# Another order of banks, reads, taps and late low parts in the head and first triple of a short-convolution block

## The chip, the cores and the metric

One core of a Trainium2 chip runs the whole program. The metric is the device time of one execution in microseconds (us), the median of several runs; lower is better. The engines are named as in the profile: PE is TensorE's matrix multiplier and PEld its weight load, DVE is VectorE, ACT is ScalarE, POOL is GpSimd, and SP is SyncE, which only starts transfers here.

## The reference

The input x has 1024 rows of 1024 channels in float32. With DEPTH 1 only the short-convolution mixer runs, between two RMS norms:

```python
def rms_norm(x, g):
    xf = x.astype(jnp.float32)
    y = xf * lax.rsqrt(jnp.mean(xf * xf, axis=-1, keepdims=True) + EPS)
    return (y * g.astype(jnp.float32)).astype(x.dtype)

def short_conv_mixer(u, w_in, conv_w, w_out):      # w_in 1024 x 8192, conv_w 3 x 2048, w_out 2048 x 1024
    z, bg, cg, v = jnp.split(u @ w_in.astype(u.dtype), 4, axis=-1)
    y = bg * causal_dwconv(cg * v, conv_w) * jax.nn.silu(z)
    return y @ w_out.astype(u.dtype)

h = x
u = rms_norm(h, pre_norm[0])
h = h + rms_norm(short_conv_mixer(u, sc_w_in[0], sc_conv_w[0], sc_w_out[0]), post_norm[0])
```

`causal_dwconv` is a convolution over positions with three taps for each of the 2048 channels.

## The kernel before, in words

**Precision.** Every float32 operand of a matmul is split into a high part (rounded to the format that PE multiplies, by a copy on ScalarE) and a low part (the rest, by a subtraction on VectorE). A product is three passes: low weights by high data, high by low, high by high (`pass3`, lines 122 to 125). So each operand needs one ScalarE and one VectorE instruction for each half ahead of its product.

**Work.** The first projection has 64 groups of 128 columns: 16 channel blocks c, each with the types CG, V, Z and BG. The four groups of c = 0 (numbers 0 to 3: CG, V, Z, BG) are made by plain products in the head, `plain(n, h, ks)` for group n and half h of the 1024 positions. The other 60 groups go three at a time: 20 triples, each made by 20 products of combined weights and combined data in place of 24, with the combinations by additions. The products are numbered 0 to 19. The combined data of product i is `U[i]`, made once in the head and in triple 0 and kept for all triples; seven of them are plain blocks `B[g, h]` (g the quarter of the input channels, h the half of the positions), the others are sums of blocks, called forms here. The combined weights come from POOL's sixteen small steps `sums(t, steps)` and are split in pairs by ScalarE and VectorE: units A to J (`split_w`, lines 208 to 225), each for two products. After the triples comes the output projection.

**Order.** The order of the instructions on each engine is that of the program text; nothing is reordered, so an instruction that waits holds everything behind it on its engine. Tiles come from pools with a fixed number of slots. The next tile of a pool, in the order of the text, takes the slot that came free first, and its first write waits until the last user of the slot's former tile is done. Two pools matter: the eight PSUM banks (`bank`), and `up` with 18 slots for operands, each as large as one `U[i]`. Instructions of two engines on one bank follow each other in program order, reads too.

**The head (lines 603 to 763).** It norms x, turns it (`turn`, `turn2`: transposes into banks `pk`), splits each block (`read_k(k, h)`: ScalarE's line 479 the high part, VectorE's line 480 the low one), writes blocks back over x for the forms (`rebuild` on POOL, `rebuild_a` on ScalarE, line 489), and makes the forms. A form is held in two banks (`form`, `banks_of`) until its high part `high_u(i)` (line 559 from banks, 561 from a stage) and its low part `low_u(i)` (lines 567 and 569) are made, or is written to a stage. A stage is half a tile of the `up` pool (`PLACE` says which half of which tile); it keeps the forms 10, 4, 0, 16, 17 and 2 until there is time for their split in triple 0. Form 19's stage is a tile of the raw pool. `snap` copies a plain result out of its bank, group 2 with a Silu. `first_tap` and `other_taps` (lines 284 to 292) are the convolution of c = 0, on ScalarE and VectorE.

**Triple 0.** The loop at lines 828 to 863 goes through the steps s = 1 to 20. In each step come, in this order: the six matmuls of one product (`ORDER_0`: 7, 9, 1, 8, 3, 5, 14, 18, 0, 13, 17, 6, 4, 11, 15, 16, 10, 2, 12, 19); the reads of its bank into the three results (`read`, lines 334 to 355, a first read on ScalarE and later ones on VectorE); the low parts that are pending, first those of the splits and then those of the operands; the leftovers of c = 0 (`first_chunk`); in five steps the high part of the next operand of `LATE` (4, 16, 10, 2, 19), whose low part becomes pending; the split of a unit (`SPLIT_0` for this triple, `NEXT` for the coming one, A at step 15); and POOL's sums for the next triple. Products of one chain (`CHAINS`) add up in one bank, so a product waits until the reads of the product before it in its chain are done: 1, 5, 18, 11, 10, 12, 19 share bank pX; 9, 3, 17, 4, 15, 16 share pY; 7, 8, 14 share pV; 6 and 2 share pZ; 0 and 13 share pW.

Of the kernel before, what the change touches and what calls it, by code (L numbers as in the profile page):

```python
# [19 lines left out]
def kernel(  # L20
# [11 lines left out]
    nc = tc.nc  # L32
# [4 lines left out]
    NK = D // P  # L37
# [121 lines left out]
    def sums(t, steps):  # L159

        if t >= len(TRIPLES):
            return
        w0, w1, w2 = (ws[t, j] for j in range(3))
        if t not in es:
            es[t] = EP[t % 2].tile([P, 6, FC], F32, tag="e", name=f"e_{t}")
        e = es[t]
        add, sub = nc.gpsimd.tensor_add, nc.gpsimd.tensor_sub
        todo = {
            0: lambda: (add(w2[:, 0], w2[:, 0], w2[:, 1]), add(w2[:, 2], w2[:, 1], w2[:, 2])),  # L169
            1: lambda: sub(e[:, 0:2], w2[:, 0::2], w0[:, 0::2]),  # L170
            2: lambda: sub(e[:, 2], e[:, 1], w0[:, 3]),
            3: lambda: add(w1[:, 2], w2[:, 2], w1[:, 2]),
            4: lambda: sub(e[:, 3], w1[:, 2], w1[:, 0]),
            5: lambda: (sub(w0[:, 2], e[:, 3], w0[:, 2]), sub(w0[:, 0], e[:, 3], w0[:, 0])),  # L174
            6: lambda: sub(w0[:, 2], w0[:, 2], w0[:, 3]),
            7: lambda: sub(e[:, 4], w2[:, 1], w2[:, 3]),
            8: lambda: sub(e[:, 5], e[:, 4], w1[:, 3]),
            9: lambda: add(w2[:, 3], w1[:, 3], w2[:, 3]),
            10: lambda: sub(w1[:, 3], w1[:, 3], e[:, 2]),
            11: lambda: sub(w2[:, 3], e[:, 0], w2[:, 3]),  # L180
            12: lambda: sub(e[:, 3], e[:, 5], w1[:, 0]),  # L181
            13: lambda: add(w1[:, 0], w1[:, 0], w1[:, 1]),
            14: lambda: sub(e[:, 2], e[:, 0], w0[:, 3]),
            15: lambda: sub(w0[:, 3], w0[:, 3], w0[:, 1]),
        }
        for s in steps:
            todo[s]()
# [16 lines left out]
    def run_lows():  # L204
        while lows:
            lows.pop(0)()
# [39 lines left out]
    def inner(t):  # L246
        return t[:, TAPS - 1 :]
# [46 lines left out]
    def pad(c):  # L294
        nc.gpsimd.tensor_copy(gts[c, 1][:, : TAPS - 1], gts[c, 0][:, HB:])
# [177 lines left out]
    def read_k(k, h):  # L473

        g, kk = k // 2, k % 2
        if kk == 0:
            B[g, h] = new_u(f"b{g}{h}")
        u, src, gc = B[g, h], pk[k, h], gcol[:, k : k + 1]
        nc.scalar.activation(u[:, 0, kk], src, AF.Copy, scale=gc)
        nc.vector.scalar_tensor_tensor(u[:, 1, kk], src, gc, u[:, 0, kk].bitcast(F32), op0=ALU.mult, op1=ALU.subtract)  # L480
# [30 lines left out]
    def plain(n, h, ks):  # L511

        w = plain_w[n]
        for k in ks:
            first = (n, h) not in plain_ps
            if first:
                plain_ps[n, h] = bank(f"pp_{n}_{h}")
                plain_k[n, h] = 0
            plain_k[n, h] += 1
            hi, lo = (w[:, z, k * P : (k + 1) * P] for z in (0, 1))  # L520
            pass3(plain_ps[n, h], hi, lo, B[k // 2, h], k % 2, first, plain_k[n, h] == NK)

    def snap(n, h, gate=False):
        t = wide(snp, "sn", f"sp_{n}_{h}")
        if gate:
            gts[0, h] = t
        nc.scalar.activation(inner(t), plain_ps[n, h], AF.Silu if n == 2 else AF.Copy)
        return inner(t)
# [4 lines left out]
                turn(k, t)  # L533

    STAGE = {}
    PLACE = {10: (0, 0), 4: (0, 1), 0: (1, 0), 16: (1, 1), 6: (2, 0), 17: (2, 1), 11: (3, 0), 2: (3, 1)}

    def stage(i):
        if i == 19:
            if i not in STAGE:  # L540
                STAGE[i] = raw.tile([P, 2, HB], F32, tag="raw", name="s_19")
            return as_block(STAGE[i])
        n, j = PLACE[i]
        if n not in STAGE:
            STAGE[n] = up.tile([P, 2, 2, HB], F32, tag="u", name=f"s_{n}")
        return as_block(STAGE[n][:, j])
# [3 lines left out]
    def form(i, make, at=None):  # L550
        FORM[i] = at or [bank(f"f_{i}_{kk}") for kk in range(2)]
        for kk in range(2):
            make(by_tile(FORM[i][kk]), kk)

    def high_u(i):
        U[i] = u = new_u(f"u_{i}")
        for kk in range(2):
            if i in FORM:
                nc.scalar.copy(u[:, 0, kk], FORM[i][kk])
            else:  # L560
                nc.scalar.copy(as_block(u[:, 0])[:, kk], stage(i)[:, kk])
# [10 lines left out]
    def make(eng, dst, kind, a, b):  # L572

        for kk in range(2):
            d, x, y = (z[kk] if isinstance(z, list) else z[:, kk] for z in (dst, a, b))
            (eng.tensor_add if kind == "+" else eng.tensor_sub)(d, x, y)
# [12 lines left out]
    def turned(k, n, other, op):  # L589

        def do(dst, kk):
            nc.vector.scalar_tensor_tensor(dst, by_tile(pk[k + kk, 1]), n[:, k + kk : k + kk + 1], other[:, kk], op0=ALU.mult, op1=op)

        return do
# [74 lines left out]
    nc.scalar.mul(half_of(cw, 1), half_of(pc[:, : TAPS * NC], 1), -1.0)  # L669
    for k in (4, 5):  # L670
        read_k(k, 1)
    form(7, turned(4, gcol, b20, ALU.subtract))
    for k in (4, 5):
        rebuild_a(k, 1)
# [12 lines left out]
    low_u(5)  # L687
    high_u(8)
    low_u(8)
    plain(3, 0, range(NK))  # L690
    turn2((0, 1))
    for k in (0, 1):
        read_k(k, 1)
# [11 lines left out]
    plain(0, 1, (0, 1))  # L705
    turn2((2, 3))
    sn0[3] = snap(3, 0)
    for k in (6, 7):
        rebuild_a(k, 1)
    for k in (2, 3):  # L710
        read_k(k, 1)
    plain(1, 1, (0, 1))
    plain(0, 1, (6, 7, 2, 3))
    plain(1, 1, (6, 7, 2, 3))
# [15 lines left out]
    f6 = banks_of(6)  # L730
    make(nc.vector, f6, "-", b01, f19)
    high_u(6)
    make(nc.vector, stage(17), "+", f6, b30)
    nc.vector.tensor_mul(cv_of(0, 1), plain_ps[1, 1], cv_of(0, 1))
    f11 = banks_of(11)
# [3 lines left out]
    FORM.pop(19)  # L739
    FORM.pop("q")  # L740
    low_u(6)
    nc.gpsimd.tensor_mul(inner(gts[0, 0]), inner(gts[0, 0]), sn0[1])
    pad(0)
    head.close()
    EP[1] = mixed.enter_context(tc.tile_pool(name="ep1", bufs=1, reuse_waits="tile"))
    wp = mixed.enter_context(tc.tile_pool(name="wp", bufs=1, reuse_waits="tile"))
    tmp = mixed.enter_context(tc.tile_pool(name="tmp", bufs=1, reuse_waits="tile"))
    for unit in "ABCD":
        split_w(0, unit)
        run_lows()  # L750
        if unit == "B":
            low_u(11)
    sums(0, range(12, 16))
    for i in (0, 17):
        high_u(i)
        low_u(i, nc.gpsimd)
    first_tap(0, 0)
    first_tap(0, 1)
    other_taps(0, 0)
    other_taps(0, 1)  # L760
    silu1 = snap(2, 1)
    for i, (g, h) in ((1, (2, 1)), (3, (3, 0)), (14, (1, 0)), (13, (1, 0)), (18, (0, 0)), (15, (1, 1)), (12, (1, 1))):
        U[i] = B[g, h]
    LATE = [4, 16, 10, 2, 19]

    def first_chunk(s):

        if s == 3:
            for h, t in ((0, sn0[2]), (1, silu1)):
                nc.gpsimd.tensor_mul(cv_of(0, h), cv_of(0, h), t)  # L770
        elif s == 9:
            gate_y(0, 0, sn0[3], 1, False)
        elif s == 10:
            gate_y(0, 1, plain_ps[3, 1], 1, True)
# [46 lines left out]
    END = len(TRIPLES) - 1  # L821
    SUMS = {1: (0,), 2: (1,), 3: (2,), 4: (3,), 5: (4,), 6: (5,), 7: (6,), 8: (7,), 9: (8,), 10: (9,), 11: (10,), 12: (11,), 17: (12, 13), 18: (14,), 19: (15,)}
    SPLIT = {2: "E", 6: "F", 8: "G", 9: "H", 11: "I", 13: "J"}
    SPLIT_0 = {1: "F", 4: "G", 7: "H", 8: "E", 11: "I", 13: "J"}
    NEXT = {15: "A", 16: "B", 18: "C", 20: "D"}
    ORDER_0 = (7, 9, 1, 8, 3, 5, 14, 18, 0, 13, 17, 6, 4, 11, 15, 16, 10, 2, 12, 19)
    fetch_triple(1)
    for t in range(len(TRIPLES)):
        for s, i in enumerate(ORDER if t else ORDER_0, 1):
            now[0] += 1  # L830
            product(t, i)
            read(t, i)
            run_lows()
            while low_us:
                low_us.pop(0)()
            if t == 0:
                first_chunk(s)
                if s in (4, 7, 10, 12, 14):
                    n = LATE.pop(0)
                    high_u(n)  # L840
                    low_us.append(lambda n=n: low_u(n))
            run_due()
            for unit in (SPLIT if t else SPLIT_0).get(s, ""):
                split_w(t, unit)
            for unit in NEXT.get(s, ""):
                split_w(t + 1, unit)
            sums(t + 1, SUMS.get(s, ()))
            if s == 14:
                fetch_triple(t + 2)
            if s in (7, 14, 20):  # L850
                run_later()
            if 2 <= t < 2 + 2 * CH:
                j = (t - 2) // 2
                if t % 2 == 0 and s == 3:
                    fetch_t(j)
                if t % 2 == 0 and s == 15:
                    add_t(j, 0)
                if t % 2 == 1 and s in (15, 20):
                    add_t(j, 1 + (s == 20))
            if t == END - 1 and s == 14 or t == END and s in (2, 8, 13, 15, 17):  # L860
                fetch_unit()
            if t == END and s in (6, 9, 11, 13, 15, 17, 19, 20):
                split_unit(True)
# [150 lines left out]
```

## Time and profile before

| | |
|---|---|
| time, median of 3 runs | 778.89 us (777.88 to 779.18) |
| the profiled execution | 776.99 us, of which the span of the trace is 775.2 us |
| granted clock of PE over the span | 0.999 |
| head, 0 to 65.2 us of the span | PE busy 62.44 us, DVE 50.11, ACT 46.13, POOL 30.81 |
| triple 0, 65.2 to 97.4 us | PE busy 28.72 us, DVE 25.56, ACT 22.84, POOL 25.99 |
| the rest, 97.4 to 775.2 us | PE busy 670.61 us, DVE 410.54, ACT 382.09, POOL 401.61 |

How to read what follows: times in a view are microseconds from the start of the span, unless marked ns. A line number such as L569 is a line of the kernel before; where a helper issues an instruction, it is the helper's line. `x2` at the end of a timeline row means two instructions in a row that the view merged. `[0.54 <-DVE u L569]` says that the engine was idle for 0.54 us before the row, and that the semaphore that ended this came from DVE's line 569, which wrote a tile u. Tiles are named without their numbers: u are operands, b blocks, s stages, f forms in banks, wA to wJ the split weights, pX to pZ the banks of the chains.

### The profile page before, as it was taken

The page shows a single profiled execution, that of the slowest core. Times are in us where ns is not written, and L with a number is a line of the kernel's source. Part 1 is how long each engine was busy: PE and PEld are TensorE (multiplying, and loading weights), DVE is VectorE, ACT ScalarE, POOL GpSimd, SP SyncE. Part 2 cuts the span into 40 slices and gives each one's busy share as a digit, 9 for nine tenths or more (in the row PEclk, how much of TensorE's full clock was granted, in tenths as well). Part 3 has the DMA queues.
Part 4 walks back from the last instruction along what each step waited for, and adds up shares of the span by engine and source line. Part 5 has one row for each costly group of instructions (what it writes and reads, how often), then busy time and mean ns, then how long its engine had stood idle before and what let it go on. Part 6 is the DMA issues. An engine that isn't in the chain of part 4 may idle for free.

```text
span 775.2 us, 10034 instructions
## 1 busy us (share of the span) xinstructions
PE 761.8 (98%) x3394; PEld 628.3 (81%) x3394; DVE 486.2 (63%) x752; ACT 451.1 (58%) x877; POOL 458.4 (59%) x563
## 2 busy tenths in 40 slices
PE   9998999999999999999999999999999999999996
PEld 8786788888888888888888888888888888888885
DVE  6887866556566475656565665555665957544756
ACT  7859575556666565555665755565566636444531
POOL 0677688679679677776977887796874220000020
PEclk9999999999999999999999999999999999999999
DMA  9400424546436448266266466565544779754237
GB/s 335 128 1 28 135 67 153 120 136 151 108 109 162 128 105 213 59 179 134 82 150 176 106 155 133 138 163 109 150 93 133 232 247 378 280 186 176 93 121 259
DMA packets 103219, 116.55 MB, mean 150 GB/s; under 512 B 4680, under 2 KB 70272, under 8 KB 102144
## 3 DMA queue, kind: packets, MB, share of 16 engines
q1 hardware_dynamic: 93936, 99.13, 38.9%
q0 software_dynamic: 9216, 16.78, 13.9%
q8 instruction: 26, 0.43, 0.2%
q14 instruction: 25, 0.20, 0.1%
q10 hardware_dynamic: 16, 0.00, 0.0%
HBM read 97.02 MB, written 44.04 MB: 182 GB/s over the span
## 4 chain that ended last, share of the span: by engine, by line
PE 91%; ACT 5%; DVE 3%; issue 1%; DMA 0%; DVEq 0%; ACTq 0%
PE pX L123 8%; PE pX L125 8%; PE pX L124 8%; PE pY L123 7%; PE pY L125 7%; PE pY L124 7%; PE po_x L892 4%; PE po_x L893 4%; PE po_x L891 4%; PE pV L123 3%; PE pV L125 3%; PE pV L124 3%; PE pZ L125 2%; PE pZ L123 2%; PE pZ L124 2%; PE pW L125 2%
## 5 line engine op out<-in xcount | busy, mean ns | idle before, releaser
L931 POOL TENSOR_TENSOR res<-xr,res 128x512 f32<-128x512 f32 x4 | 6.9, 1720 | 105.5 <-DVE res L930 105.5
L329 POOL TENSOR_TENSOR g<-g,sn 128x512 f32<-128x512 f32 x29 | 40.2, 1391 | 45.5 <-ACT sn L327 35.2
L353 DVE TENSOR_TENSOR sn<-sn,pY 128x512 f32<-128x512 f32 x57 | 39.2, 688 | 36.2 <-PE pY L125 20.7
L353 DVE TENSOR_TENSOR sn<-sn,pX 128x512 f32<-128x512 f32 x57 | 39.2, 689 | 34.5 <-PE pX L125 34.5
L302 POOL TENSOR_TENSOR g<-sn,g 128x512 f32<-128x512 f32 x23 | 29.9, 1302 | 47.4 <-DVE sn L351 47.4
L327 ACT ACTIVATE sn<-sn 128x512 f32<-128x512 f32 x24 | 15.2, 633 | 64.1 <-DVE sn L353 40.1
L311 POOL TENSOR_TENSOR g<-g,sn 128x512 f32<-128x512 f32 x20 | 28.3, 1415 | 17.9 <-DVE sn L353 17.6
L345 ACT COPY sn<-pZ 128x512 f32<-128x512 f32 x19 | 11.2, 590 | 46.4 <-PE pZ L125 41.3
L347 ACT ACTIVATE sn<-pV 128x512 f32<-128x512 f32 x38 | 20.7, 600 | 28.5 <-PE pV L125 28.5
L169 POOL TENSOR_TENSOR raw<-raw 128x256 f32<-128x256 f32 x40 | 32.6, 933 | 0.0
L359 POOL DMA_DIRECT2D s_d<-s_d x24 | 19.8, 823 | 21.0 <-DMA s_d<-y_d 13.5
L174 POOL TENSOR_TENSOR raw<-e,raw 128x256 f32<-128x256 f32 x40 | 28.8, 741 | 1.6
L351 DVE TENSOR_TENSOR g<-pY,g 128x512 f32<-128x512 f32 x15 | 10.4, 692 | 30.7 <-PE pY L125 30.7
L123 PE MATMUL pp<-b,wn 128*128 128x512 f32 x64 | 26.0, 406 | 1.1 <-DVE u L567 1.0
L170 POOL TENSOR_TENSOR e<-raw,raw 128x512 f32<-128x512 f32 x20 | 25.9, 1295 | 1.6
L900 ACT ACTIVATE jk<-res 128x512 bf16<-128x512 f32 x12 | 7.6, 632 | 32.0 <-DVE res L958 13.0
L181 POOL TENSOR_TENSOR e<-e,raw 128x256 f32<-128x256 f32 x20 | 14.8, 742 | 18.9 <-ACT wB L219 18.9
L124 PE MATMUL pp<-b,wn 128*128 128x512 f32 x64 | 25.2, 394 | 0.6 <-DVE b L480 0.6
L125 PE MATMUL pp<-b,wn 128*128 128x512 f32 x64 | 25.0, 390 | 0.0
L292 DVE SCALAR_TENSOR_TENSOR g<-g,cw,cv 128x512 f32<-128x512 f32 x30 | 22.5, 749 | 1.7
L224 DVE TENSOR_TENSOR wD<-wD,wD 128x512 fp32r<-128x512 f32 x20 | 13.7, 684 | 14.3 <-ACT wD L223 14.3
L292 DVE SCALAR_TENSOR_TENSOR cv<-g,cw,cv 128x512 f32<-128x512 f32 x30 | 22.4, 748 | 0.0
(373 smaller groups left out, 2902.7 us busy)
## 6 DMA issues: line engine op xcount, KB each, us to landing
raw<-in_sc_w_in SPq DMA_DIRECT2D x64, 512.0 KB, 4.4
t_d<-in_sc_w_out SPq DMA_DIRECT2D x32, 256.0 KB, 4.8
s_d<-g SPq DMA_DIRECT2D x29, 256.0 KB, 2.1
s_d<-s_d POOLq DMA_DIRECT2D x24, 256.0 KB, 4.4
y_d<-g SPq DMA_DIRECT2D x23, 256.0 KB, 2.5
t_d<-in_sc_w_out POOLq DMA_DIRECT2D x16, 256.0 KB, 7.8
t_d<-t_d POOLq DMA_DIRECT2D x16, 256.0 KB, 4.3
xr<-in_x SPq DMA_DIRECT2D x8, 512.0 KB, 4.6
```

Of the source, the lines that this page charges most:

```text
L123: nc.tensor.matmul(ps, lo, u[:, 0, kk], start=first, stop=False, skip_group_check=True)
L124: nc.tensor.matmul(ps, hi, u[:, 1, kk], start=False, stop=False, skip_group_check=True)
L125: nc.tensor.matmul(ps, hi, u[:, 0, kk], start=False, stop=last, skip_group_check=True)
L169: 0: lambda: (add(w2[:, 0], w2[:, 0], w2[:, 1]), add(w2[:, 2], w2[:, 1], w2[:, 2])),
L174: 5: lambda: (sub(w0[:, 2], e[:, 3], w0[:, 2]), sub(w0[:, 0], e[:, 3], w0[:, 0])),
L292: nc.vector.scalar_tensor_tensor(g if j == TAPS - 1 else ps, g, tap(c, j), ps, op0=ALU.mult, op1=ALU.add)
L302: nc.gpsimd.tensor_mul(g, src, g)
L329: when([(c, "cv", h), (c, "silu", h)], (c, "z", h), {"cv": 1, "silu": 1}, lambda: nc.gpsimd.tensor_mul(cv_of(c, h), cv_of(c, h), t))
L353: nc.vector.tensor_sub(a, a, ps)
L891: nc.tensor.matmul(ps, lo, u[:, 0, k % 2], start=first, stop=False, skip_group_check=True)
L892: nc.tensor.matmul(ps, hi, u[:, 1, k % 2], start=False, stop=False, skip_group_check=True)
L893: nc.tensor.matmul(ps, hi, u[:, 0, k % 2], start=False, stop=last, skip_group_check=True)
```

## The change

It changes order and places only; the arithmetic is the same.

- `PLACE`: form 2 moves to the free half of the tile that form 17 uses (its other half was kept for form 6, which is never staged), and the tile that form 2 shared with a place for form 11 is no longer made.
- The plain products of group 3, first half, stand ahead of form 7 in the text, so their bank is taken before those of forms 7, 9 and 8. PE's own order is unchanged by this.
- `read_k(2, 1)` and `read_k(3, 1)` stand ahead of `rebuild_a(6, 1)` and `rebuild_a(7, 1)`.
- POOL's gate of c = 0, first half, and its `pad` stand earlier in the text.
- The taps of the first half stand ahead of split A (the first tap) and behind A's low part (the others); those of the second half stand ahead of the splits of `U[0]` and `U[17]`.
- The Silu of group 2, second half (`snap(2, 1)`), moves from the end of the head to step 2 of triple 0, and POOL's products with the two Silus from step 3 to step 4.
- In triple 0, unit H is split at step 5 instead of 7 and E at step 7 instead of 8; the five high parts of `LATE` come at steps 7, 9, 11, 13, 15 instead of 4, 7, 10, 12, 14.

```diff
--- before.py
+++ after.py
@@ -533,7 +533,7 @@
                 turn(k, t)
 
     STAGE = {}
-    PLACE = {10: (0, 0), 4: (0, 1), 0: (1, 0), 16: (1, 1), 6: (2, 0), 17: (2, 1), 11: (3, 0), 2: (3, 1)}
+    PLACE = {10: (0, 0), 4: (0, 1), 0: (1, 0), 16: (1, 1), 2: (2, 0), 17: (2, 1)}
 
     def stage(i):
         if i == 19:
@@ -669,6 +669,7 @@
     nc.scalar.mul(half_of(cw, 1), half_of(pc[:, : TAPS * NC], 1), -1.0)
     for k in (4, 5):
         read_k(k, 1)
+    plain(3, 0, range(NK))
     form(7, turned(4, gcol, b20, ALU.subtract))
     for k in (4, 5):
         rebuild_a(k, 1)
@@ -687,7 +688,6 @@
     low_u(5)
     high_u(8)
     low_u(8)
-    plain(3, 0, range(NK))
     turn2((0, 1))
     for k in (0, 1):
         read_k(k, 1)
@@ -705,10 +705,10 @@
     plain(0, 1, (0, 1))
     turn2((2, 3))
     sn0[3] = snap(3, 0)
+    for k in (2, 3):
+        read_k(k, 1)
     for k in (6, 7):
         rebuild_a(k, 1)
-    for k in (2, 3):
-        read_k(k, 1)
     plain(1, 1, (0, 1))
     plain(0, 1, (6, 7, 2, 3))
     plain(1, 1, (6, 7, 2, 3))
@@ -730,6 +730,8 @@
     f6 = banks_of(6)
     make(nc.vector, f6, "-", b01, f19)
     high_u(6)
+    nc.gpsimd.tensor_mul(inner(gts[0, 0]), inner(gts[0, 0]), sn0[1])
+    pad(0)
     make(nc.vector, stage(17), "+", f6, b30)
     nc.vector.tensor_mul(cv_of(0, 1), plain_ps[1, 1], cv_of(0, 1))
     f11 = banks_of(11)
@@ -739,34 +741,36 @@
     FORM.pop(19)
     FORM.pop("q")
     low_u(6)
-    nc.gpsimd.tensor_mul(inner(gts[0, 0]), inner(gts[0, 0]), sn0[1])
-    pad(0)
     head.close()
     EP[1] = mixed.enter_context(tc.tile_pool(name="ep1", bufs=1, reuse_waits="tile"))
     wp = mixed.enter_context(tc.tile_pool(name="wp", bufs=1, reuse_waits="tile"))
     tmp = mixed.enter_context(tc.tile_pool(name="tmp", bufs=1, reuse_waits="tile"))
+    first_tap(0, 0)
     for unit in "ABCD":
         split_w(0, unit)
         run_lows()
+        if unit == "A":
+            other_taps(0, 0)
         if unit == "B":
             low_u(11)
     sums(0, range(12, 16))
+    first_tap(0, 1)
+    other_taps(0, 1)
     for i in (0, 17):
         high_u(i)
         low_u(i, nc.gpsimd)
-    first_tap(0, 0)
-    first_tap(0, 1)
-    other_taps(0, 0)
-    other_taps(0, 1)
-    silu1 = snap(2, 1)
     for i, (g, h) in ((1, (2, 1)), (3, (3, 0)), (14, (1, 0)), (13, (1, 0)), (18, (0, 0)), (15, (1, 1)), (12, (1, 1))):
         U[i] = B[g, h]
     LATE = [4, 16, 10, 2, 19]
 
+    silu1 = []
+
     def first_chunk(s):
 
-        if s == 3:
-            for h, t in ((0, sn0[2]), (1, silu1)):
+        if s == 2:
+            silu1.append(snap(2, 1))
+        elif s == 4:
+            for h, t in ((0, sn0[2]), (1, silu1[0])):
                 nc.gpsimd.tensor_mul(cv_of(0, h), cv_of(0, h), t)
         elif s == 9:
             gate_y(0, 0, sn0[3], 1, False)
@@ -821,7 +825,7 @@
     END = len(TRIPLES) - 1
     SUMS = {1: (0,), 2: (1,), 3: (2,), 4: (3,), 5: (4,), 6: (5,), 7: (6,), 8: (7,), 9: (8,), 10: (9,), 11: (10,), 12: (11,), 17: (12, 13), 18: (14,), 19: (15,)}
     SPLIT = {2: "E", 6: "F", 8: "G", 9: "H", 11: "I", 13: "J"}
-    SPLIT_0 = {1: "F", 4: "G", 7: "H", 8: "E", 11: "I", 13: "J"}
+    SPLIT_0 = {1: "F", 4: "G", 5: "H", 7: "E", 11: "I", 13: "J"}
     NEXT = {15: "A", 16: "B", 18: "C", 20: "D"}
     ORDER_0 = (7, 9, 1, 8, 3, 5, 14, 18, 0, 13, 17, 6, 4, 11, 15, 16, 10, 2, 12, 19)
     fetch_triple(1)
@@ -835,7 +839,7 @@
                 low_us.pop(0)()
             if t == 0:
                 first_chunk(s)
-                if s in (4, 7, 10, 12, 14):
+                if s in (7, 9, 11, 13, 15):
                     n = LATE.pop(0)
                     high_u(n)
                     low_us.append(lambda n=n: low_u(n))
```

## The prediction

> **What bounds the kernel now.** I read the page first, for the share of each engine and the span, and then asked where PE is not fed: PE's own waits, and its timeline at those places.
>
> ```profile
> span 775.2 us, 10034 instructions
> ## 1 busy us (share of the span) xinstructions
> PE 761.8 (98%) x3394; PEld 628.3 (81%) x3394; DVE 486.2 (63%) x752; ACT 451.1 (58%) x877; POOL 458.4 (59%) x563
> ```
>
> PE is busy for 98% of the span, so only PE's gaps are to be had. PE's waits, in the first 140 us (name <- who ended the wait, then total, times, longest, in us), lie in the head and the first triple:
>
> ```profile
> PE pX L123 <- DVE g L351: 2.0, 1, 2.0
> ...
> PE pp L123 <- DVE u L567: 1.0, 1, 1.0
> PE pV L123 <- ACT gc L347: 0.8, 1, 0.8
> PE pY L123 <- DVE wE L224: 0.7, 1, 0.7
> ```
>
> The timeline of PE (start, duration, line, and in brackets the idle time before it) gives each place its price, since matmuls in a full stream start at even distances:
>
> ```profile
> 33.15 0.39 PE L125 MATMUL pp<-b,wn 128*128 128x512 f32 x1
> 34.48 0.47 PE L123 MATMUL pp<-b,wn 128*128 128x512 f32 x1 [0.95 <-DVE u L567]
> 34.79 0.40 PE L124 MATMUL pp<-b,wn 128*128 128x512 f32 x1
> ...
> 49.54 0.49 PE L123 MATMUL pp<-b,wn 128*128 128x512 f32 x1
> 50.32 0.50 PE L124 MATMUL pp<-b,wn 128*128 128x512 f32 x1 [0.29 <-DVE b L480]
> 50.65 0.39 PE L125 MATMUL pp<-b,wn 128*128 128x512 f32 x1
> ...
> 65.23 0.39 PE L123 MATMUL pV<-u,wA 128*128 128x512 f32 x1
> ...
> 66.59 0.39 PE L123 MATMUL pY<-u,wB 128*128 128x512 f32 x1
> ...
> 97.44 0.39 PE L123 MATMUL pV<-u,wA 128*128 128x512 f32 x1
> ```
>
> One product (six matmuls) takes 66.59 - 65.23 = 1.36 us, one matmul 0.23. The row at 65.23 is product 7 at step 1 of triple 0, the row at 97.44 the same of triple 1: 32.21 us for 20 products, where 20 x 1.36 = 27.2 would do. So triple 0 loses 5.0 us. In the head, 33.15 to 34.48 to 34.79 is 1.10 + 0.08 over the even distance, and 49.54 to 50.32 to 50.65 is 0.55 + 0.10: 1.83 us. All that this change can win is 6.8 us.
>
> **The head, part by part.** The stall at 34.48 is a bank: the first matmul of `plain(3, 0)` is ended by DVE's line 567, `low_u(7)`, which reads a bank of form 7. The new order asks for the bank of `plain(3, 0)` ahead of form 7, when one is long free. No PE instruction lies between the old and the new place, so PE's order stays; its weights' low part was made before form 7. I take the whole 1.18 us. What is late next: `turn2((0, 1))` and the reads behind it start 1.2 us sooner, and DVE, which runs without a break up to `low_u(8)`, starts these reads nearly as much sooner. Form 8's two banks now wait for `low_u(7)`, but ScalarE copies into them just as that ends: nothing.
>
> The stall at 50.32 is the low half of operand 2: ScalarE runs `rebuild_a(6)`, `rebuild_a(7)`, which wait for VectorE's `stage(4)`, before `read_k(2)`. With the reads in front, VectorE can go from `stage(4)` straight to `read_k(2)`, and the rebuilds follow; they are next used by form 19, behind form q on VectorE. I take 0.65; if this cover went, VectorE's form 19 would wait, not PE. Together 1.83: step 1 starts at 65.23 - 1.83 = 63.40.
>
> The free slot: `stage(2)` now shares a tile with `stage(17)`, so it needs no slot of a third operand that `plain(2, 1)` still reads. VectorE no longer waits there, and the splits A to D, whose memory is that of the head's x, start earlier on ScalarE. With one first tap in front of them and the Silu of `snap(2, 1)` moved behind the reads of product 7, these reads come ahead of product 8: the pV wait goes. In step 4 `low_u(4)` no longer runs, which had held up the read of product 5:
>
> ```profile
> 74.80 2.73 DVE L569 TENSOR_TENSOR u<-s,u 128x512 fp32r<-128x512 f32 x2
> ...
> 85.86 1.98 DVE L569 TENSOR_TENSOR u<-s,u 128x512 fp32r<-128x512 f32 x2
> 87.77 0.68 DVE L224 TENSOR_TENSOR wI<-wI,wI 128x512 fp32r<-128x512 f32 x1
> 88.37 0.67 DVE L353 TENSOR_TENSOR gc<-gc,pY 128x512 f32<-128x512 f32 x1
> 88.97 1.28 DVE L569 TENSOR_TENSOR u<-s,u 128x512 fp32r<-128x512 f32 x2
> ```
>
> The first row is that `low_u(4)`: 2.73 us, and the pX wait of 2.0 us follows it. H (step 5) and E (step 7) are split one to two steps ahead of their products. So I see no PE wait in steps 1 to 10, and step 10 ends at 63.40 + 10 x 1.36 = 77.00.
>
> POOL's gate of the first half is written earlier in the program, but nothing of POOL lies between: free. Its two silu products go from step 3 to 4, behind one more step of sums; their users come at steps 9 and 10: free. On SP, the last load of `fetch_triple(2)` takes the slot of form 19's stage, freed when `low_u(19)` ends, and is used by POOL in triple 1: at most a microsecond later, and ten steps ahead of the split that would feel it.
>
> **The late low parts.** Here the change adds a chain. `high_u(10)` takes the slot of the tile that `low_u(16)` reads last, `high_u(2)` that of `low_u(10)`, `high_u(19)` that of `low_u(2)`. That holds today too, as ScalarE's timeline shows at 87.88:
>
> ```profile
> 84.69 1.13 ACT L561 CAST u<-s 128x512 fp32r<-128x512 f32 x2
> ...
> 86.24 0.62 ACT L219 CAST wI<-raw 128x512 fp32r<-128x512 f32 x1
> 87.88 1.14 ACT L561 CAST u<-s 128x512 fp32r<-128x512 f32 x2 [0.54 <-DVE u L569]
> ...
> 89.74 0.59 ACT L223 CAST wJ<-wJ 128x512 fp32r<-128x512 f32 x1
> 90.28 1.14 ACT L561 CAST u<-s 128x512 fp32r<-128x512 f32 x2
> ...
> 92.19 0.59 ACT L223 CAST wA<-wA 128x512 fp32r<-128x512 f32 x1
> ```
>
> But with the high parts at steps 7, 9, 11, 13, 15 instead of 4, 7, 10, 12, 14, each low part falls into a step whose split's low part stands ahead of it on VectorE: `low_u(10)` behind I's, `low_u(2)` behind J's, `low_u(19)` behind A's. So it waits for ScalarE's high part and its split as well. ScalarE's pairs last 84.69 to 86.86 (high 10 and I), 2.17; 87.88 to 90.33 (2 and J), 2.45; 90.28 to 92.78 (19 and A), 2.50. A low part of a split takes 0.60 from start to start (87.77, 88.37, 88.97), as does a read.
>
> A `low_u` pair takes 1.28 at 88.97 and 1.98 at 85.86. Beside the second, POOL is slowed as well:
>
> ```profile
> 85.41 0.74 POOL L178 TENSOR_TENSOR raw<-raw,raw 128x256 f32<-128x256 f32 x1
> 86.23 1.06 POOL L179 TENSOR_TENSOR raw<-raw,e 128x256 f32<-128x256 f32 x1
> 87.26 1.19 POOL L180 TENSOR_TENSOR raw<-e,raw 128x256 f32<-128x256 f32 x1
> ```
>
> So I take 1.98 where POOL still works at its twelve sums of triple 1 (the pairs 4, 16 and 10) and 1.28 where it has none (2). For 19, which now runs when split B lets POOL go on with sum 12, I take the middle, 1.63. The Trainium skill, SBUF — State Buffer, section Who interferes with whom, says that a VectorE instruction with two SBUF inputs contends with a GpSimd instruction that reads SBUF, and that the other is blocked rather than slowed. The rows agree in kind; if each half waited out one whole POOL sum of 0.74, an estimate by that page would be 2.76 a pair and the sum below some 3 us later.
>
> The chain, with 0.05 for each handover (87.84 to 87.88): step 8 ends at 74.28; the read of 18 starts 0.2 later (a matmul's row outlasts its 0.23 by 0.16), with E's low part it fills 1.2; `low_u(4)` runs from 75.68 to 77.66; the read of 13 takes 0.6; `low_u(16)` from 78.2 to 80.2; ScalarE's 10 and I to 82.4; I's low part; `low_u(10)` from 83.05 to 85.05; ScalarE's 2 and J to 87.55; J's low part; `low_u(2)` from 88.2 to 89.5; ScalarE's 19 and A to 92.05; A's low part; `low_u(19)` from 92.7 to 94.3; then, behind it on VectorE, the read of product 10, 0.67, for which product 12 at step 19 must wait, since both use bank pX. Step 19 starts at 95.0, triple 1 at 95.0 + 2 x 1.36 = 97.75, against 97.44 today. On the way the read of 17 stands behind `low_u(16)` and the read of 4 behind `low_u(10)`, so products 4 and 15 wait too, some 1.5 us each; the wait at step 19 is about 4 us. The 6.8 us won are returned. From triple 1 on nothing changes, and the order there is the old one: +0.3 us in the profile's own terms, 776.99 (the span 775.2 and 1.8 around it) to 777.3; that execution lies 1.9 under the median of 778.89, so I predict **779.2 us**.
>
> **The rivals.** *The gaps close and stay closed.* If some slot or order spares the chain, all 6.8 us remain: 778.9 - 6.8 = 772.1. For it: VectorE is busy 63% only. Against: the waits come from order and latency, not from load. The Trainium skill, Perfetto Trace Analysis, section Optimization Strategy, has this as its rule: find the gaps of the most contended engine and make what they wait for start sooner. By that rule one gets this rival's time; no run here shows yet that a filled gap stays filled. Chance 0.10.
>
> *The chain is free of POOL.* With 1.28 for every pair, `low_u(4)` is hidden by the read of 13, which then starts at 77.2, 0.4 sooner; 16 and 10 give 0.7 each, 19 gives 0.35: 2.15 sooner, 1.85 under today: 777.0, just beyond what can be told. Against it: POOL has its twelve sums in that time. Chance 0.14.
>
> *Slower: POOL's wide instructions.* `low_u(4)` cost 2.73 at 74.80, beside the two 512-wide silu products of POOL. These, and the 512-wide gate of step 9, can again fall on pairs 4, 16 or 10: 0.75 more for each of two, and 0.35 for 19: +1.85 on the forecast, +2.1 on today, 781.0. It decides once the four pairs take some 1.2 us more than I charged. A new PE wait before step 10, say a read of 5 that comes late for product 18, would end the same way. Chance 0.31.
>
> **How the numbers follow.** A measurement here tells about 0.2%, 1.56 us, from no change. The forecast, with its own range of 777.4 to 780.4, has 0.45. Faster: 0.10 + 0.14 = 0.24; within: 0.45; slower: 0.31. The range 776.8 to 781.2 leaves out the closed gaps and the far end of the slower case.
>
> **What would show it.** Step 1 of triple 0 near 63.4 with no PE wait at `plain(3, 0)` or at `read_k(2)`'s low half; step 10 ending near 77.0; then PE waits at products 4 (on line 353, the read of 17), 15 and, the longest, 12; DVE idle in front of the low parts of I, J and A, ended by ScalarE. If product 12 starts well under 93, the chain is wrong; if PE waits before step 10, the first half is.

## The result, and the profile after

The changed kernel takes 779.54 us, the median of 13 executions (778.83 to 780.44). The kernel before took 777.89 us beside it on the same chip (776.99 to 779.18). The ratio is 1.0022, with an interval of 1.0014 to 1.0031: slower by 1.65 us, about the 0.2% that can be told at all. The profiled execution of after took 779.52 us.

Its page has the span and the engines:

```profile
span 777.7 us, 10030 instructions
## 1 busy us (share of the span) xinstructions
PE 762.4 (98%) x3394; PEld 630.7 (81%) x3394; DVE 485.8 (62%) x752; ACT 450.1 (58%) x877; POOL 457.9 (59%) x563
```

Nothing was added to any engine; the span is 2.5 us longer because PE stands still, or runs slowly, somewhere else. The waits of PE in the first 140 us (total, times, longest), and PE's busy time in the 15 us from about the start of triple 0 (columns after the stretch: its length, then busy time and instructions of PE, PEld, DVE, ACT and POOL, then PE's granted clock, the DMA share and GB/s):

```profile
PE pX L123 <- DVE gc L353: 3.7, 1, 3.7
PE pY L123 <- DVE gc L353: 2.6, 2, 1.3
...
63.00:78.00 15.00, 15.00 (x68) 12.44 (x67) 10.62 (x16) 12.00 (x25) 14.32 (x15) 1.00 0.12 37
```

The waits at `plain(3, 0)`, at `read_k(2)`'s low half and those on pV, on wE and on `DVE g L351` are gone. PE is busy for all of the 15 us in which steps 1 to 10 fall. In their place stand three waits on reads (line 353), two of 1.3 us (products 4 and 15) and one of 3.7. PE's timeline at that last one, which is product 12 at step 19, goes on to the first product of triple 1:

```profile
95.11 0.50 PE L123 MATMUL pX<-b,wJ 128*128 128x512 f32 x1 [3.71 <-DVE gc L353]
95.45 0.51 PE L124 MATMUL pX<-b,wJ 128*128 128x512 f32 x1
95.75 0.63 PE L125 MATMUL pX<-b,wJ 128*128 128x512 f32 x1
96.18 0.63 PE L123 MATMUL pX<-b,wJ 128*128 128x512 f32 x1
...
98.74 0.51 PE L123 MATMUL pX<-u,wJ 128*128 128x512 f32 x1
99.09 0.40 PE L124 MATMUL pX<-u,wJ 128*128 128x512 f32 x1
...
99.56 0.39 PE L123 MATMUL pV<-u,wA 128*128 128x512 f32 x1
```

Read the distances of the starts. From the third matmul behind the wait on they start 0.43 us apart, not 0.23, and each lasts 0.63, not 0.39. The same stretch by windows shows why:

```profile
95.10:99.00 3.90, 3.89 (x10) 3.09 (x11) 1.75 (x3) 0.00 (x0) 2.60 (x3) 0.56 0.47 134
```

PE is busy throughout, with ten matmuls where 17 would fit: the granted clock is 0.56 on average (in steps of 0.05 us it is 0.50 from 95.57 to 98.99, and 1.00 before and behind). Two products take 99.56 - 95.11 = 4.45 us instead of 2.72.

What product 12 waited for is seen on VectorE and on ScalarE. VectorE:

```profile
75.83 1.87 DVE L569 TENSOR_TENSOR u<-s,u 128x512 fp32r<-128x512 f32 x2
...
78.23 1.82 DVE L569 TENSOR_TENSOR u<-s,u 128x512 fp32r<-128x512 f32 x2
...
82.96 2.01 DVE L569 TENSOR_TENSOR u<-s,u 128x512 fp32r<-128x512 f32 x2
...
87.54 0.69 DVE L224 TENSOR_TENSOR wJ<-wJ,wJ 128x512 fp32r<-128x512 f32 x1 [1.37 <-ACT wJ L223]
88.15 1.28 DVE L569 TENSOR_TENSOR u<-s,u 128x512 fp32r<-128x512 f32 x2
...
92.04 0.69 DVE L224 TENSOR_TENSOR wA<-wA,wA 128x512 fp32r<-128x512 f32 x1 [2.00 <-ACT wA L223]
92.64 1.82 DVE L569 TENSOR_TENSOR u<-s,u 128x512 fp32r<-128x512 f32 x2
94.38 0.67 DVE L353 TENSOR_TENSOR gc<-gc,pX 128x512 f32<-128x512 f32 x1
```

ScalarE, the first cast of the pair 2 and the last cast of A:

```profile
85.06 1.14 ACT L561 CAST u<-s 128x512 fp32r<-128x512 f32 x2 [2.26 <-DVE u L569]
...
91.42 0.59 ACT L223 CAST wA<-wA 128x512 fp32r<-128x512 f32 x1
```

The two engines take turns: ScalarE waits 2.26 us for VectorE's `low_u(10)` to free the slot (the row at 82.96), casts 2 and J; VectorE, idle for 1.37, is then given J's low part and `low_u(2)`; then ScalarE again. At the end stands `low_u(19)`, and behind it the read at 94.38 that product 12 needs. From `low_u(16)` at 78.23 to `low_u(19)` at 92.64 this chain takes 14.41 us. In the kernel before, the same two rows lay 10.29 us apart:

```profile
81.08 1.83 DVE L569 TENSOR_TENSOR u<-s,u 128x512 fp32r<-128x512 f32 x2
...
91.37 1.28 DVE L569 TENSOR_TENSOR u<-s,u 128x512 fp32r<-128x512 f32 x2
```

### The profile page after: what moved, and what is told of

It is laid out like the page before. It is cut to its first block, busy times and chain, and to the rows that moved or that the text cites. A ratio compares the mean times of both kernels' runs of the same rounds, so it can differ in the third digit from the quotient of the medians.

```text
span 777.7 us, 10030 instructions
## 1 busy us (share of the span) xinstructions
PE 762.4 (98%) x3394; PEld 630.7 (81%) x3394; DVE 485.8 (62%) x752; ACT 450.1 (58%) x877; POOL 457.9 (59%) x563
## 4 chain that ended last, share of the span: by engine, by line
PE 91%; ACT 3%; DVE 2%; DMA 2%; issue 0%; POOLq 0%; POOL 0%; SPq 0%; DVEq 0%; ACTq 0%
PE pX L123 8%; PE pX L125 8%; PE pX L124 8%; PE pY L123 7%; PE pY L125 7%; PE pY L124 7%; PE pV L123 3%; PE pV L125 3%; PE pV L124 3%; PE po_x L897 3%; PE po_x L896 3%; PE po_x L895 3%; PE pZ L123 2%; PE pZ L125 2%; PE pZ L124 2%; PE pW L123 2%
## 5 line engine op out<-in xcount | busy, mean ns | idle before, releaser
L351 DVE TENSOR_TENSOR g<-pY,g 128x512 f32<-128x512 f32 x15 | 10.4, 692 | 30.7 <-PE pY L125 30.7
```

## The experiments

**Is it the chain, and is it the order that makes it?** The theory: the late steps of the high parts, together with VectorE's order (split first, late operand behind it), make the chain some 4 us longer. The rival: POOL's instructions make the pairs long. The first two experiments shorten the chain in two independent ways, and leave POOL's work as it is. The first undoes the late steps:

```diff
-                if s in (7, 9, 11, 13, 15):
+                if s in (4, 7, 10, 12, 14):
```

> The changed kernel with one part undone: the high parts of LATE at steps 4, 7, 10, 12, 14 again. Theory (chain): the change's 6.8 us came back as waits behind the late low parts, which with steps 7 to 15 stand behind the low parts of I, J and A. With the old steps low_u(10), low_u(2) and low_u(19) run one step ahead of those; low_u(4) at step 5 delays the read of 5 and product 18 by 1.3 to 2 us, step 19 waits 0.5 us at most, no slow restart: triple 1 starts near 93, 4 us ahead of the kernel before, about 774 us. Rival (POOL): the low parts are slow because POOL works beside them, wherever they stand, and moving them only moves the wait: within 1.5 us of the kernel before, or of the changed one.

Measured: 772.97 us (772.89 to 773.26), ratio to before 0.9940 (0.9927 to 0.9952). PE's waits, and the pairs 4, 16, 10 and 19 on VectorE:

```profile
PE pX L123 <- DVE g L351: 1.1, 1, 1.1
...
PE pY L123 <- DVE gc L353: 0.6, 1, 0.6
...
71.40 2.01 DVE L569 TENSOR_TENSOR u<-s,u 128x512 fp32r<-128x512 f32 x2
...
76.96 2.05 DVE L569 TENSOR_TENSOR u<-s,u 128x512 fp32r<-128x512 f32 x2
...
80.82 2.46 DVE L569 TENSOR_TENSOR u<-s,u 128x512 fp32r<-128x512 f32 x2
...
87.39 1.28 DVE L569 TENSOR_TENSOR u<-s,u 128x512 fp32r<-128x512 f32 x2
```

The first three pairs are not shorter than in after (one takes 2.46), yet from 16 to 19 the chain takes 87.39 - 76.96 = 10.43 us, and no wait is over 1.1. The second leaves the late steps and turns VectorE's order round in triple 0: the late operand ahead of the split's low part.

```diff
             read(t, i)
+            if t == 0:
+                while low_us:
+                    low_us.pop(0)()
             run_lows()
```

> The changed kernel with one exchange: in triple 0 VectorE does the pending operand low part of a step ahead of the splits' low part. Steps of LATE as in the change (7 to 15), POOL as in the change. Chain: ScalarE's split between two low_u pairs drops out of the chain; waits of 0.6 to 0.9 us at products 17, 4, 15 and 12 in place of 1.3, 1.3 and 3.7, and no slow restart: triple 1 starts near 93.7, about 774 us, 5 us under the changed kernel. POOL rival: each of the pairs 4, 16 and 10 still runs beside POOL at 1.8 to 2.0 us, so at most 1 us is gained: 778.5 us or more.

Measured: 773.97 us (773.69 to 774.15), ratio 0.9950 (0.9937 to 0.9964). The pairs 16, 10 and 19:

```profile
78.39 1.97 DVE L569 TENSOR_TENSOR u<-s,u 128x512 fp32r<-128x512 f32 x2
...
81.48 2.44 DVE L569 TENSOR_TENSOR u<-s,u 128x512 fp32r<-128x512 f32 x2
...
88.88 1.28 DVE L569 TENSOR_TENSOR u<-s,u 128x512 fp32r<-128x512 f32 x2
```

The chain starts as late as in after (78.39 against 78.23) and takes 88.88 - 78.39 = 10.49 us. So neither the late steps alone nor the pairs' lengths make the 14.4 us; it takes the late steps behind the split-first order. The third puts the late steps, and nothing else of the change, into the kernel before:

```diff
-                if s in (4, 7, 10, 12, 14):
+                if s in (7, 9, 11, 13, 15):
```

> The kernel before with one part of the change alone: LATE at steps 7, 9, 11, 13, 15. Chain: the 2 us pX wait at product 18 goes, as low_u(4) no longer stands ahead of the read of 5, but then the chain from step 10 on makes product 12 wait some 4 us with a slow restart behind it: triple 1 starts near 103, 5 to 6 us slower than the kernel before, 783 us. Rival (the loss belongs to the head's new order or to the shared stage, not to LATE): 2 us faster than before, 776 us.

Measured: 783.15 us (782.62 to 784.43), ratio 1.0071 (1.0059 to 1.0084). The pX wait of 2.0 us at product 18 goes, and this comes:

```profile
PE pX L123 <- DVE gc L353: 3.7, 1, 3.7
PE pY L123 <- DVE gc L353: 2.0, 2, 1.4
```

The one line costs 783.15 - 777.28 = 5.9 us in the kernel before (777.28 on that chip), and in the changed one, by the ratios to before, 1.0022 - 0.9940 of 777.3, that is 6.4 us; the slow stretch, priced next, is part of both. It alone turns the change from a gain into a loss.

**What is the slow stretch behind the wait worth?** Sixteen matmuls on operands that are long ready, into the unused bank pd, fill the wait of product 12. They leave the wait's end where it is, and PE busy.

```diff
+            if t == 0 and i == 12:
+                pd, wd = bank("pd"), B[1, 0]
+                for _ in range(16):
+                    nc.tensor.matmul(pd, wd[:, 0, 0, :P], wd[:, 0, 1], start=True, stop=True, skip_group_check=True)
             product(t, i)
```

> The changed kernel with 16 more matmuls (128 x 512, into a bank that nothing reads) in front of product 12 in triple 0: 16 x 0.23 = 3.6 us of work in the 3.7 us in which PE waits there. The semaphore wait is the same. Theory (clock): the ten matmuls after that wait started 0.43 us apart because the clock was granted at 0.56 after an idle PE; kept busy, PE starts them 0.23 apart: product 12 again at 95.1, triple 1 at 97.9 in place of 99.56, 1.6 us under the changed kernel. Rival (those matmuls are slow from what VectorE and POOL do then, or from late weight loads): no change, or slower by what the fillers overrun.

Measured: 777.70 us (777.42 to 778.41, 11 executions), ratio to before 1.0004 (0.9995 to 1.0013). PE's timeline, and the window:

```profile
91.29 3.79 PE L838 MATMUL pd<-b 128*128 128x512 f32 x16
95.22 0.50 PE L123 MATMUL pX<-b,wJ 128*128 128x512 f32 x1
95.56 0.40 PE L124 MATMUL pX<-b,wJ 128*128 128x512 f32 x1
...
98.11 0.39 PE L123 MATMUL pV<-u,wA 128*128 128x512 f32 x1
...
95.00:99.00 4.00, 3.86 (x17) 3.11 (x17) 1.96 (x4) 0.69 (x2) 2.66 (x4) 1.00 0.47 135
```

Product 12 starts no sooner (95.22), the clock stays at 1.00, the two products take 2.89 us instead of 4.45: 1.56 us in this view; by the ratios (1.0022 and 1.0004) 1.4, between the medians 1.84. With more work on PE the kernel is faster. Three more kernels fill only a part of the wait, to see how long it must be:

```diff
-                for _ in range(16):
+                for _ in range(2):      # then 4, then 6
```

> After, with 2 of the 16 filling matmuls in the wait of product 12: the wait shrinks from 3.71 to about 3.25 us, product 12 starts at 95.1 as before. Length theory (TensorE's clock is taken down when it has stood idle for somewhat more than 3 us): still or nearly still slow, matmuls 0.43 apart, 779.0 to 779.5. Rival, that the clock is taken down by any wait over 2 us: the same here. Rival, that any filling at all, by ending the idle stretch in between, keeps the clock: 777.7.

> After, with 4 filling matmuls: the wait shrinks to about 2.8 us. Length theory: the matmuls of product 12 start 0.23 apart, triple 1 starts at 98.1 and not at 99.6, 777.7. Rival (any wait over 2 us): still slow, 779.5.

> After, with 6 filling matmuls: the wait shrinks to about 2.3 us, near the 2.0 us before product 18 of the kernel before, behind which the clock was full. Both theories: full clock or nearly always so, 777.7; a slow stretch here would say that the length of the wait does not decide.

Measured: 779.16, 779.16 and 778.50 us. None of the theories holds through all three. The waits left were 3.26, 2.83 and 2.38 us, and in the profiled executions it was the middle one that was slow. PE's timeline with four:

```profile
94.94 0.80 PE L123 MATMUL pX<-b,wJ 128*128 128x512 f32 x1 [2.83 <-DVE gc L353]
95.53 0.63 PE L124 MATMUL pX<-b,wJ 128*128 128x512 f32 x1
```

With two, where the wait was longer:

```profile
94.90 0.50 PE L123 MATMUL pX<-b,wJ 128*128 128x512 f32 x1 [3.26 <-DVE gc L353]
95.24 0.39 PE L124 MATMUL pX<-b,wJ 128*128 128x512 f32 x1
```

So the length of the wait does not decide alone, and the executions of one kernel differ too. With six filling matmuls, the eleven executions fall into two groups: six with a mean granted clock of 0.998 or 0.999 at a median of 777.82 us, five with 0.996 at a median of 779.38. The groups are 1.56 us apart, the price that the timelines of after and of the filled wait gave. With four, 11 of 12 executions are in the slower group (778.68 us or more, clock 0.996 or less), with two 8 of 11 (778.94 or more), and all 13 of after took 778.83 or more. With sixteen one of 11 stands apart, at 778.41 us and 0.996. Filling less than the whole wait thus buys a chance and not a certainty.

The listed clock alone does not tell the groups apart. The profiled execution with sixteen lists 0.997 at 777.62 us: its clock is full at product 12 and 0.50 from 771.4 us on, behind PE's last matmul, where it costs nothing. And the kernel before, whose longest wait was 2.0 us, has slower executions too: beside these three kernels 7 of its 29 executions took 778.80 to 779.08 us, against a median of 777.66. None of these seven was profiled, so whether they lose their time behind that wait is not shown.

**The head.** The two edits of the head alone, in the kernel before:

```diff
+    plain(3, 0, range(NK))
     form(7, turned(4, gcol, b20, ALU.subtract))
...
-    plain(3, 0, range(NK))
     turn2((0, 1))
...
-    for k in (6, 7):
-        rebuild_a(k, 1)
     for k in (2, 3):
         read_k(k, 1)
+    for k in (6, 7):
+        rebuild_a(k, 1)
```

> The kernel before with the two moves in the head alone: the plain products of group 3 asked for ahead of form 7, and read_k(2), read_k(3) ahead of rebuild_a(6), rebuild_a(7). If the head is PE's alone, the 1.83 us of the two waits arrive whole, as everything behind them moves forward: step 1 at 63.4, and 1.8 us under the kernel before, 775.5 us. Rival: the waits of triple 0 are set by ScalarE and VectorE, which do not move, and take it back at products 8 and 18: no change.

Measured: 775.38 us (775.13 to 776.96, 10 executions), ratio 0.9974 (0.9965 to 0.9984): 2.2 us under the 777.61 of before on that chip. Step 1 starts at 63.44, against 65.23. The waits of triple 0 stay as they were:

```profile
PE pX L123 <- DVE g L351: 2.0, 1, 2.0
...
PE pV L123 <- ACT gc L347: 0.8, 1, 0.8
...
PE pY L123 <- DVE wE L224: 0.7, 1, 0.7
```

What is won in the head stays won: triple 1 starts at 95.64, 1.80 sooner than before.

**The shared stage.** The changed kernel with the old places of the stages:

```diff
-    PLACE = {10: (0, 0), 4: (0, 1), 0: (1, 0), 16: (1, 1), 2: (2, 0), 17: (2, 1)}
+    PLACE = {10: (0, 0), 4: (0, 1), 0: (1, 0), 16: (1, 1), 6: (2, 0), 17: (2, 1), 11: (3, 0), 2: (3, 1)}
```

> The changed kernel with the old places: form 2 in a tile of its own, whose slot VectorE must wait for until plain(2, 1) has ended (58.3). Chain: VectorE's stage(2) and ScalarE's splits come 1.2 us later, which the slack ahead of steps 1 to 7 mostly hides; pV waits 0.3 at product 8 with 0.1 to restart, and the chain from step 10 is later by as much: 0.4 to 0.6 us over the changed kernel, 780. Rival (the freed slot is what took the waits of steps 4 to 11 away): pV 0.8 and pX 1 us or more return, 781 or more.

Measured: 780.25 us (779.37 to 781.36), ratio 1.0034 (1.0021 to 1.0047), which the interval of after (1.0014 to 1.0031) overlaps. The wait itself comes back on VectorE, ahead of a stage:

```profile
58.57 1.29 DVE L576 TENSOR_TENSOR s<-f,xa 128x512 f32<-128x512 f32 x2 [1.39 <-PE pp L125]
```

The wait at product 8 that was expected with it did not come; PE lost 0.20 us at product 7. The rest of the change covers most of what the held slot costs.

**Fewer sums on POOL.** Of POOL's sums in triple 0 for the weights of triple 1, numbers 3, 5, 6, 9, 10 and 11 are left out, so the weights of triple 1 are incomplete.

```diff
-            sums(t + 1, SUMS.get(s, ()))
+            sums(t + 1, [n for n in SUMS.get(s, ()) if t or n not in (3, 5, 6, 9, 10, 11)])
```

> The changed kernel without seven of POOL's sums for triple 1 (steps 3, 5, 6, 9, 10 and 11 are left out, so the weights of triple 1 are not the right combinations); order and waits of all else as in the change. This prices POOL's part in the chain. If the pairs 4, 16 and 10 take 1.87, 1.82 and 2.01 us because POOL reads at the same time, two or three of them come down to 1.3 to 1.5: product 12 starts 1 to 1.7 us sooner, its wait falls to 2 to 2.7 us, and if that spares the slow clock, another 1.6 us: 776 to 777 us. If POOL is no cause, the pairs stay and it is 779.5.

Measured: 779.10 us (777.14 to 780.65, 8 executions), ratio 1.0019 (1.0008 to 1.0030), no less than after within the intervals. The forecast, 776 to 777, missed (its text says seven sums; it is these six). What POOL still had to do moved forward, onto the pairs that were to be freed; VectorE's pairs 16 and 10, then POOL:

```profile
78.16 2.32 DVE L569 TENSOR_TENSOR u<-s,u 128x512 fp32r<-128x512 f32 x2
...
83.39 1.28 DVE L569 TENSOR_TENSOR u<-s,u 128x512 fp32r<-128x512 f32 x2
```

```profile
77.05 1.74 POOL L311 TENSOR_TENSOR sp<-sp,sp 128x512 f32<-128x512 f32 x1
78.75 1.18 POOL L177 TENSOR_TENSOR e<-e,raw 128x256 f32<-128x256 f32 x1
92.83 0.73 POOL L181 TENSOR_TENSOR e<-e,raw 128x256 f32<-128x256 f32 x1 [12.90 <-ACT wB L219]
```

Only pair 10 ran beside an idle POOL: 1.28 us instead of 2.01. That is the price of POOL for one pair, shown; pair 16 gave 0.50 of it back (2.32 instead of 1.82). Product 12 started at 94.76, 0.35 sooner than in after, but in the profiled execution the clock then stayed at 0.50 for 6.8 us (93.81 to 100.64), twice as long as in after, so triple 1 started at 100.05, against 99.56. What a chain wholly free of POOL would take was not measured.

**The best version.** From the first experiment, with the high part of 4 one step earlier still, and the low part of a split held back one step at steps 12 and 16:

```diff
             read(t, i)
-            run_lows()
+            if t or s not in (12, 16):
+                run_lows()
...
-                if s in (7, 9, 11, 13, 15):
+                if s in (3, 7, 10, 12, 14):
```

> The version with the old steps of LATE, taken further: the first high part at step 3 in place of 4, and the splits' low parts of steps 12 and 16 held back by one step, so that the reads of 4 and 10 do not stand behind them. Chain: the three waits left in that version (1.1 at product 18, 0.6 at 15, 0.2 at 12, with their restarts 2.8 us in all) shrink to 0.2, 0.3 and 0.4 with 0.3 for restarts, 1.5 us less: about 771.5 us. If VectorE's total work is what bounds triple 0 now, nothing is gained: 773.

Measured: 771.77 us (771.73 to 772.03), ratio 0.9925 (0.9911 to 0.9939), the fastest of all. Triple 1 starts at 92.12, 5.3 us sooner than before. In triple 0 two waits are left, the second of them new, at product 10 (step 17):

```profile
PE pX L123 <- DVE gc L353: 0.6, 1, 0.6
...
PE pX L123 <- ACT u L561: 0.4, 1, 0.4
```

## Why the prediction was right, and where it was short

Forecast 779.2, measured 779.54; but against the kernel before, +0.3 was forecast and +1.65 measured. That the number came out so near is in part luck. The forecast was laid on the median of the kernel before over three executions, 778.89 us; over the thirteen beside after it is 777.89. This 1.0 us too much made up for 1.0 of the 1.35 us by which the loss was forecast too small. Step by step:

**The head, 1.83: right.** Step 1 starts at 63.55 (forecast 63.40); the profiled execution of after is 0.23 later already at the first matmul of the head (13.01 against 12.78). Alone, the two edits gave 1.8 us in the timeline and 2.2 between the medians.

**No PE wait in steps 1 to 10: right.** Step 10 ends at 77.15 (77.00). Of the cause only a part is shown: with the stages in their old places, VectorE's wait comes back but hardly any wait of PE, so the free slot that the prediction named first for it is not what closes these gaps. The pX wait at product 18 is the late steps' doing: with these alone it goes (the third experiment), and with the old ones 1.1 us of it comes back (the first). Which edit closed the gaps on pV and wE was not separated.

**The chain of late low parts: right, place and price.** `low_u(4)` at 75.83 (75.68), `low_u(16)` at 78.23 (78.2), `low_u(10)` at 82.96 (83.05), `low_u(2)` at 88.15 (88.2), `low_u(19)` at 92.64 (92.7), product 12 at 95.11 (95.0); the waits 1.27, 1.31 and 3.71 where 1.5, 1.5 and 4 were said. The five pairs took 8.80 us in all; 1.98 x 3 + 1.28 + 1.63 = 8.85 had been charged (0.27 too much on 4 and 16 met 0.22 too little on 10 and 19). Its cause, the late steps behind the split-first order, is shown twice, by the first and the second experiment: 10.4 and 10.5 us from 16 to 19 instead of 14.4.

**"Triple 1 at 95.0 + 2 x 1.36 = 97.75": this step failed.** Behind a wait of 4 us it charged two products at full speed. They took 4.45 us, and triple 1 started at 99.56. Of the 1.73 us over 2.72, 1.56 are the granted clock, shown by the filled wait, and 0.17 the restart that the filled wait pays as well. That is nearly the whole difference at triple 1: 0.3 + 1.7 = 2.0 against 99.56 - 97.44 = 2.12. Of the 2.5 us by which the span is longer, the other 0.4 lies behind the start of triple 1; this rest of the span differs by up to 0.45 us among the traces here (677.69 to 678.14 us). For its waits in triple 0 the prediction charged nothing beyond their length: the restart of 0.08 and 0.10 us that it had read in the head is not in this sum, and a lower clock is in none of its sums or rivals.

**The rivals.** The gaps that close and stay closed, 772.1: not what the change does, but what it would do without its one line on the late steps (772.97), or with the order of the best version (771.77). The chain free of POOL, 777.0: the price per pair was right (1.28 against 2.01), the condition not met. Slower by POOL's wide instructions, 781.0: wrong in its mechanism. No pair was longer than 2.01 us in after, where it needed two at 2.73; the loss came at the restart of PE instead. In the first two experiments the pairs were longer (2.46 and 2.44) and cost little.

## What to carry to other kernels

A gap that is closed ahead of a chain of reused slots is given back unless the chain starts earlier too or gets shorter. Work out when each holder of a slot is freed, and what stands ahead of the freeing instruction in its engine's queue: here one line of start steps was worth 6.4 us, and turning two pieces of work round on VectorE 5.6 (1.0022 - 0.9950 of 777.3). Charge a wait of TensorE of 3.7 us with a slow stretch behind it (here 1.56 us), and treat it as a chance for waits of 2.4 to 3.3 us, perhaps from some 2 us on; the last section says what the chance hangs on.

## What the runs showed of the hardware

The granted clock fell to 0.50 behind or within a long wait, and for a time that did not depend on the work: read in steps of 0.05 us, it was 0.50 for 3.41 us in after (95.57 to 98.99), in the run with four filling matmuls (94.43 to 97.85, so from within the wait on) and in the runs of the third experiment and of the shared stage, and for 6.83 us, twice as long, in the run with fewer sums. The Trainium skill, TensorE: Matmul & The Clock Gate, Part 1: The HAM clock gate, says that the clock is halved after an idle window of about 3.4 us, that such windows run freely, and that a busy one restores it. The runs agree in the halving, in the 3.41 us, and in that the same wait is punished in some executions only.

They agree in the free running as well. In each of these five traces the clock falls once more near the end, behind PE's last matmul, and from the first fall to that one it is 199 or 200 times 3.4133 us, to within 0.01 us (in after 95.57 and 774.83, 679.25 us apart), whatever PE did between. So the one fall at the end of any trace places the windows at product 12. In the five traces with a slow stretch the window that ended at the fall held 3.41, 2.95, 2.75, 2.74 and 2.32 us of idle PE (third experiment, after, fewer sums, shared stage, four filling matmuls). With two filling matmuls an edge between two windows, at 93.30, cut the wait of 3.26 us into 1.66 and 1.60, with six one at 94.48 cut 2.38 into 1.59 and 0.79, and in the kernel before one at 77.34 cut the 1.96 at product 18 into 1.12 and 0.84: the clock stayed full. Behind the last matmul of the program, windows with 2.21 us idle (the first experiment) brought the fall and windows with 1.76 (the kernel before) did not.

So here the runs differ from the page in one condition: a window need not be idle throughout. In all thirteen traces 2.2 us or more of idle PE in one window took the clock down, and 1.8 us or less never did. By that, the place of the wait in the windows makes it a chance, and it is certain only for a wait so long that no edge can cut it into two harmless parts. A wait was never moved against the windows on purpose; this is read off the traces as they fell. The 6.83 us fit as well: the second window of that run held 0.95 us of the wait and did not restore the clock, while windows with 0.51 us (four filling matmuls) and 0.27 us (third experiment) did.
